# Batched x times y-transposed in groups of four heads: one 4 MB store a group in 32 KB rows, with weight tiles of 32 columns, in place of two 2 MB stores in 16 KB rows with 64 columns

## The chip, the cores and the metric

The kernel runs on one NeuronCore of a Trainium2 chip. The metric is the device time of one execution in microseconds (us), lower is better; the time before is the median of 5 runs. The profile is of one of those executions. The core has a TensorE (PE, with its weight loads as PEld), VectorE (DVE), ScalarE (ACT), GpSimd (POOL), SyncE (SP, which here only issues DMAs) and 16 DMA engines that move data between the device memory (HBM) and the on-chip memory (SBUF). PE writes to PSUM, from where DVE or ACT copy to SBUF.

## The reference

```python
batch, n_heads, seq_t, seq_s, channels = 8, 12, 512, 512, 64
x: (8, 12, 512, 64) float32      # b h t c
y: (8, 12, 512, 64) float32      # b h s c

def reference(x, y):
    return np.einsum('bhtc,bhsc->bhts', x, y).astype(np.float32)
```

For each of the 96 heads it is a 512 x 64 matrix times a 64 x 512 matrix. The inputs are 25.2 MB together, the output 100.7 MB.

## The kernel before

The 96 heads are taken in 24 groups (NG) of four heads (G = 4). In memory a group of x, y or of the output is one contiguous block. It is cut over the 128 partitions so that partition p holds rows 16p to 16p + 15 (R = 16) of the group's 4 x 512 rows: 32 partitions (Q = 32) for each head, 16 rows in each. For x and y that is 4 KB a partition (xv, yv).

Loads: `load(g)` (L51 to L56) issues two DMAs of 512 KB on SP, y first. The first six groups are loaded at the start (L58), the load of group g + 6 is issued when `prepare(g)` runs (L73). The load pool has 6 buffers for each input.

`prepare(g)` (L64 to L98) is a generator that is advanced step by step between the tiles of the group before. POOL casts y to bf16 and writes every row twice, side by side (L68), and casts x to bf16 (L72). PE transposes y in 16 blocks of 128 x 128 (L81); because of the doubled rows, partitions 0 to 63 and 64 to 127 of the result hold the same channels. The two halves are copied from PSUM to yT with the order of columns changed so that the s index runs contiguously (L87 on DVE, L89 on ACT): the source is read with a stride. x is transposed in 8 blocks of two rows each (L93), so that a block k has the channels of row 2k on partitions 0 to 63 and those of row 2k + 1 on 64 to 127. The copy to xT (L94, DVE) interleaves blocks i and i + 4 as neighbouring columns, the index e, so that 64 neighbouring columns of xT are 32 partitions' rows of one head, two rows each. These are the weight tiles of the product.

The product (L106 to L130) runs for each group over two pairs of heads (hp) and in each over four steps i2. In a step four matmuls fill one PSUM tile pm of 128 x 1,024 f32: for both heads of the pair (h2) and both row parities (par), a matmul of 64 channels x 64 weight columns x 512 moving columns. `par` selects partitions 0 to 63 or 64 to 127 of xT and yT as input, and the half of pm's columns; h2 selects 64 of pm's partitions. Each of the four is thus in another quarter of the PE array. pm is then copied to the output tile ot, by ACT for even i2 (L123) and DVE for odd (L125). There are 3 buffers for pm.

ot has 8 rows (I) x 512 f32, 16 KB, a partition: a pair of heads fills all 128 partitions. The pool has 8 buffers. A filled ot is stored by one DMA of 2 MB on SP in rows of 16 KB (L130); the first ot of the kernel and the last one (`edge`) are stored in two DMAs of 1 MB, in runs of 8 KB, as soon as each half is filled (L128).

The tile framework sets the semaphores. All DMAs go through SP's queue in the order of the program: for each group two loads, then its stores. Eight semaphores take turns for the DMAs, so that a DMA is issued only when the eighth before it has landed.

Of the kernel before, what the change touches and what calls it, by code (L numbers as in the profile page):

```python
# [1 line left out]

# [5 lines left out]


@with_exitstack  # L10
def kernel(
    ctx: ExitStack,
    tc: tile.TileContext,
    x: bass.AP,
    y: bass.AP,
    out: bass.AP,
):

    nc = tc.nc
    B, H, T, C = x.shape
    _, _, S, _ = y.shape
    P = 128
    G = 4
    Q = P // G
    R = T // Q
    NG = B * H // G
    K = R // 2  # L30
    HP = 2
    I = R // 2
    fp32 = mybir.dt.float32
    bf16 = mybir.dt.bfloat16
    assert C * 2 == P and S == T and R == 16

    xv = x.rearrange("b h t c -> (b h t c)").rearrange("(g p n) -> g p n", p=P, n=R * C)
    yv = y.rearrange("b h t c -> (b h t c)").rearrange("(g p n) -> g p n", p=P, n=R * C)
    ov = out.rearrange("b h t s -> (b h t s)").rearrange("(g a p n) -> g a p n", a=G // HP, p=P, n=I * S)

    const = ctx.enter_context(tc.tile_pool(name="const", bufs=1))
    lpool = ctx.enter_context(tc.tile_pool(name="lpool", bufs=6))
    bpool = ctx.enter_context(tc.tile_pool(name="bpool", bufs=2))
    tpool = ctx.enter_context(tc.tile_pool(name="tpool", bufs=2))
    opool = ctx.enter_context(tc.tile_pool(name="opool", bufs=8))
    ptpool = ctx.enter_context(tc.tile_pool(name="ptpsum", bufs=2, space=bass.MemoryType.PSUM))
    pmpool = ctx.enter_context(tc.tile_pool(name="pmpsum", bufs=3, space=bass.MemoryType.PSUM))

    loaded = {}

    def load(g):  # L51
        xs = lpool.tile([P, R * C], fp32)
        ys = lpool.tile([P, R * C], fp32)
        nc.sync.dma_start(ys, yv[g])
        nc.sync.dma_start(xs, xv[g])
        loaded[g] = (xs, ys)  # L56

    for g in range(6):  # L58
        load(g)

    ident = const.tile([P, P], bf16)
    make_identity(nc, ident)

    def prepare(g, made):  # L64

        xs, ys = loaded.pop(g)
        yb = bpool.tile([P, R, 2, C], bf16)
        nc.gpsimd.tensor_copy(  # L68
            yb, ys.rearrange("p (r c) -> p r c", c=C).unsqueeze(2).to_broadcast([P, R, 2, C])
        )  # L70
        xb = bpool.tile([P, R * C], bf16)
        nc.gpsimd.tensor_copy(xb, xs)  # L72
        if g + 6 < NG:  # L73
            load(g + 6)
        yield
        yT = tpool.tile([P, G * Q, R], bf16)
        xT = tpool.tile([P, K // 2, P, 2], bf16)
        for half in range(2):
            pt = ptpool.tile([P, K, P], bf16)
            for k in range(K):  # L80
                nc.tensor.transpose(  # L81
                    pt[:, k, :], yb[:, half * K + k].rearrange("p a c -> p (a c)"), ident
                )
            dst = yT[:, :, half * K:(half + 1) * K]
            src = pt.rearrange("p k n -> p n k")
            if half == 0:
                nc.vector.tensor_copy(dst, src)  # L87
            else:
                nc.scalar.activation(dst, src, mybir.ActivationFunctionType.Copy)  # L89
            yield  # L90
        pt = ptpool.tile([P, K, P], bf16)
        for k in range(K):
            nc.tensor.transpose(pt[:, k, :], xb[:, k * P:(k + 1) * P], ident)  # L93
        nc.vector.tensor_copy(  # L94
            xT.rearrange("p i n e -> p i e n"), pt.rearrange("p (e i) n -> p i e n", e=2)
        )
        made[g] = (xT, yT.rearrange("p n k -> p (n k)"))
        yield  # L98

    made = {}  # L100
    for _ in prepare(0, made):
        pass
    for g in range(NG):
        xT, yT = made.pop(g)
        steps = prepare(g + 1, made) if g + 1 < NG else iter(())
        for hp in range(G // HP):  # L106
            ot = opool.tile([P, I, S], fp32)
            edge = (g == 0 and hp == 0) or (g == NG - 1 and hp == 1)
            for i2 in range(I // 2):
                if i2 % 2 == 0:  # L110
                    next(steps, None)
                pm = pmpool.tile([P, 2, S], fp32)
                for h2 in range(HP):
                    h = hp * HP + h2
                    for par in range(2):
                        nc.tensor.matmul(  # L116
                            pm[h2 * 64:(h2 + 1) * 64, par, :],
                            xT[par * C:(par + 1) * C, i2, h * Q:(h + 1) * Q, :].rearrange("c q e -> c (q e)"),
                            yT[par * C:(par + 1) * C, h * S:(h + 1) * S],
                            start=True, stop=True,  # L120
                        )
                if i2 % 2 == 0:
                    nc.scalar.activation(ot[:, 2 * i2:2 * i2 + 2, :], pm, mybir.ActivationFunctionType.Copy)  # L123
                else:
                    nc.vector.tensor_copy(ot[:, 2 * i2:2 * i2 + 2, :], pm)  # L125
                if edge and i2 % 2 == 1:
                    a, b = (2 * i2 - 2) * S, (2 * i2 + 2) * S
                    nc.sync.dma_start(ov[g, hp][:, a:b], ot.rearrange("p r s -> p (r s)")[:, a:b])  # L128
            if not edge:
                nc.sync.dma_start(ov[g, hp], ot.rearrange("p r s -> p (r s)"))  # L130


# [1 line left out]
_INS = ['x', 'y']  # L134
_OUTS = [((8, 12, 512, 512), 'float32')]


# [23 lines left out]
```

## Time and profile before

| | us |
|---|---|
| median of 5 runs | 306.88 (306.79 to 308.15) |
| the profiled execution, its own time | 306.79 |
| its span, first to last instruction | 305.0 |
| PE busy, 1,344 matmuls and transposes | 159.8 |
| PEld busy, 1,344 weight loads | 83.8 |
| DVE busy | 172.8 |
| ACT busy | 117.3 |
| POOL busy | 70.5 |
| DMA: 126.04 MB, mean over the span | 413 GB/s |
| stores of 2 MB: 46, issue to landing | 25.0 median |
| stores of 1 MB: 4, issue to landing | 23.5 median |
| loads of 512 KB: 48, issue to landing | 24.5 median |

Busy time is the time in which an engine executed something, as a sum over the span; engines work beside each other, so the rows add up to more than the span. The page divides the span into 40 slices and gives each engine's busy share in tenths, and the same for the mean of the 16 DMA engines. "share of 16 engines" for a queue is the time that its packets took, over 16 times the span. In the groups of instructions the columns are busy time, mean time of one in ns, and the idle time just before them with what ended most of it.

### The profile page before, as it was taken

To read this page: it belongs to the slowest core of one execution; us is meant where nothing else is said; L and a number is where in the kernel's file an instruction comes from. 1 tells how busy PE (TensorE), PEld (TensorE's weight loads), DVE (VectorE), ACT (ScalarE), POOL (GpSimd) and SP (SyncE) were. 2 spreads that over 40 slices of the span, in tenths; PEclk is the share of its full clock that TensorE was granted. 3 is DMA by queue.
4 is the path that set the end of the run, shared out by engine and by line. 5 is a ranking of instruction groups with operands and counts; after the bars stand their busy time and mean duration, and the time that the engine had idled before them with its cause. 6 is when DMAs were issued, how large, how long until landed. Compare 5 with 4: busy or idle time off the path is not lost.

```text
span 305.0 us, 3408 instructions
## 1 busy us (share of the span) xinstructions
PE 159.8 (52%) x1344; PEld 83.8 (27%) x1344; DVE 172.8 (57%) x144; ACT 117.3 (38%) x121; POOL 70.5 (23%) x54
## 2 busy tenths in 40 slices
PE   1887678666554665636656466465654854300000
PEld 1453334342332323413224133242332421100000
DVE  0799999766464664646646565465564775410000
ACT  1487767434234342343323523335234453400000
POOL 4864335132130321303213213032130000000000
PEclk9966666655555555555555555555555555555555
DMA  7999999999999999999999999999999999999991
GB/s 284 416 386 440 423 420 434 414 440 410 421 434 435 417 434 415 439 414 425 435 424 427 431 423 430 430 421 439 417 438 425 431 428 432 434 425 436 423 411 68
DMA packets 14127, 126.04 MB, mean 413 GB/s; under 512 B 1568, under 2 KB 1568, under 8 KB 7712
## 3 DMA queue, kind: packets, MB, share of 16 engines
q1 hardware_dynamic: 14112, 125.84, 98.0%
q8 instruction: 10, 0.16, 0.2%
q14 instruction: 5, 0.04, 0.0%
HBM read 25.17 MB, written 100.66 MB: 413 GB/s over the span
## 4 chain that ended last, share of the span: by engine, by line
DMA 78%; DVE 6%; PE 1%; ACT 1%; POOL 1%; issue 0%; SPq 0%; ACTq 0%
DMA out_dram<-ot 77%; DVE ot L125 4%; DVE xT L94 1%; DVE yT L87 1%; DMA ys<-in_y_dram 1%; PE pm L116 1%; ACT ot L123 1%; POOL yb L68 1%; PE pt L81 0%; PE pt L93 0%; SPq L130 0%; ACTq L123 0%
## 5 line engine op out<-in xcount | busy, mean ns | idle before, releaser
L125 DVE COPY ot<-pm 128x1024 f32<-128x1024 f32 x96 | 116.3, 1220 | 78.7 <-DMA out_dram<-ot 58.8
L123 ACT ACTIVATE ot<-pm 128x1024 f32<-128x1024 f32 x96 | 94.4, 1022 | 142.0 <-DMA out_dram<-ot 129.5
L116 PE MATMUL pm<-yT,xT 64*64 64x512 bf16 x768 | 97.6, 572 | 85.2 <-ACT ot L123 69.6
L68 POOL CAST yb<-ys 128x2048 bf16<-128x2048 f32 x24 | 45.4, 1893 | 135.4 <-DMA ys<-in_y_dram 114.2
L116 PEld LDWEIGHTS <-xT 64*64 64x64 bf16 x768 | 31.0, 120 | 135.2 <-issue 119.6
L81 PE MATMUL pt<-ident,yb 128*128 128x128 bf16 x384 | 45.7, 287 | 15.7 <-DVE xT L94 9.4
L81 PEld LDWEIGHTS <-yb 128*128 128x128 bf16 x384 | 36.4, 133 | 25.2 <-issue 18.6
L94 DVE COPY xT<-pt 128x1024 bf16<-128x1024 bf16 x24 | 31.2, 1299 | 9.5 <-PE pt L93 9.5
L87 DVE COPY yT<-pt 128x1024 bf16<-128x1024 bf16 x24 | 29.1, 1213 | 7.2 <-PE pt L81 7.2
L72 POOL CAST xb<-xs 128x1024 bf16<-128x1024 f32 x24 | 25.0, 1040 | 21.9 <-PE pt L93 21.9
L93 PE MATMUL pt<-ident,xb 128*128 128x128 bf16 x192 | 25.3, 287 | 6.1 <-ACT yT L89 4.5
L89 ACT ACTIVATE yT<-pt 128x1024 bf16<-128x1024 bf16 x24 | 24.7, 1028 | 7.0 <-PE pt L81 6.3
L93 PEld LDWEIGHTS <-xb 128*128 128x128 bf16 x192 | 17.4, 123 | 22.2 <-issue 21.9
L89 ACT ACT_TABLE_LOAD x1 | 1.3, 1283 | 0.7 <-PEq L145 0.7
masks.py:199 POOL TENSOR_SCALAR_AFFINE_SELECT ident<-ident 128x128 bf16<-128x128 bf16 x1 | 0.3, 292 | 0.1
masks.py:197 POOL MEMSET ident<- 128x128 bf16 x1 | 0.2, 204 | 0.3 <-POOLq L145 0.3
L145 POOL MEMSET const-float32-0.0<- 128x1 f32 x1 | 0.1, 98 | 0.2 <-issue 0.2
L145 POOL MEMSET const-bfloat16-1.0<- 128x1 bf16 x1 | 0.1, 101 | 0.0
L145 POOL MEMSET const-uint8-127<- 128x1 uint8 x1 | 0.1, 101 | 0.0
L145 POOL MEMSET const-float32-1.0<- 128x1 f32 x1 | 0.1, 98 | 0.0
## 6 DMA issues: line engine op xcount, KB each, us to landing
out_dram<-ot SPq DMA_DIRECT2D x46, 2048.0 KB, 25.0
ys<-in_y_dram SPq DMA_DIRECT2D x24, 512.0 KB, 24.6
xs<-in_x_dram SPq DMA_DIRECT2D x24, 512.0 KB, 24.4
out_dram<-ot SPq DMA_DIRECT2D x4, 1024.0 KB, 23.5
```

The lines of the kernel that those rows point to most:

```text
L68: nc.gpsimd.tensor_copy(yb, ys.rearrange("p (r c) -> p r c", c=C).unsqueeze(2).to_broadcast([P, R, 2, C]))
L72: nc.gpsimd.tensor_copy(xb, xs)
L81: nc.tensor.transpose(pt[:, k, :], yb[:, half * K + k].rearrange("p a c -> p (a c)"), ident)
L87: nc.vector.tensor_copy(dst, src)
L89: nc.scalar.activation(dst, src, mybir.ActivationFunctionType.Copy)
L93: nc.tensor.transpose(pt[:, k, :], xb[:, k * P:(k + 1) * P], ident)
L94: nc.vector.tensor_copy(xT.rearrange("p i n e -> p i e n"), pt.rearrange("p (e i) n -> p i e n", e=2))
L116: nc.tensor.matmul(pm[h2 * 64:(h2 + 1) * 64, par, :], xT[par * C:(par + 1) * C, i2, h * Q:(h + 1) * Q, :].rearrange("c q e -> c (q e)"), y ...
L123: nc.scalar.activation(ot[:, 2 * i2:2 * i2 + 2, :], pm, mybir.ActivationFunctionType.Copy)
L125: nc.vector.tensor_copy(ot[:, 2 * i2:2 * i2 + 2, :], pm)
L145: nc = _bacc.Bacc("TRN2", target_bir_lowering=False, num_devices=1)
```

## The change

The output of a group is handled as one tile instead of two. ot is now 16 rows x 512 f32, 32 KB, a partition, for all four heads; its pool has 4 buffers in place of 8, the same bytes. A group's 4 MB are stored by one DMA in rows of 32 KB; in the first group and in the last one four DMAs of 1 MB in runs of 8 KB store a quarter each as soon as it is filled.

To fill such a tile, a step k makes two rows of every partition: pm's partitions 32h to 32h + 31 hold head h. So eight matmuls fill one pm, four heads times two parities, each with 64 channels x 32 weight columns x 512 moving columns. There are 8 steps a group as before, with the same number of copies on ACT and DVE, and the same places for the steps of `prepare`. The interleaving of xT falls away: xT is a plain copy of the transposed blocks. The copies of the transposed y, which read PSUM with a stride and write contiguous rows, are the same lines in both kernels.

```diff
-    HP = 2
-    I = R // 2
...
-    ov = out.rearrange("b h t s -> (b h t s)").rearrange("(g a p n) -> g a p n", a=G // HP, p=P, n=I * S)
+    ov = out.rearrange("b h t s -> (b h t s)").rearrange("(g p n) -> g p n", p=P, n=R * S)
...
-    opool = ctx.enter_context(tc.tile_pool(name="opool", bufs=8))
+    opool = ctx.enter_context(tc.tile_pool(name="opool", bufs=4))
...
-        xT = tpool.tile([P, K // 2, P, 2], bf16)
+        xT = tpool.tile([P, K, P], bf16)
...
-        nc.vector.tensor_copy(
-            xT.rearrange("p i n e -> p i e n"), pt.rearrange("p (e i) n -> p i e n", e=2)
-        )
+        nc.vector.tensor_copy(xT, pt)
...
-        for hp in range(G // HP):
-            ot = opool.tile([P, I, S], fp32)
-            edge = (g == 0 and hp == 0) or (g == NG - 1 and hp == 1)
-            for i2 in range(I // 2):
-                if i2 % 2 == 0:
-                    next(steps, None)
-                pm = pmpool.tile([P, 2, S], fp32)
-                for h2 in range(HP):
-                    h = hp * HP + h2
-                    for par in range(2):
-                        nc.tensor.matmul(
-                            pm[h2 * 64:(h2 + 1) * 64, par, :],
-                            xT[par * C:(par + 1) * C, i2, h * Q:(h + 1) * Q, :].rearrange("c q e -> c (q e)"),
-                            yT[par * C:(par + 1) * C, h * S:(h + 1) * S],
-                            start=True, stop=True,
-                        )
...
-                if edge and i2 % 2 == 1:
-                    a, b = (2 * i2 - 2) * S, (2 * i2 + 2) * S
-                    nc.sync.dma_start(ov[g, hp][:, a:b], ot.rearrange("p r s -> p (r s)")[:, a:b])
-            if not edge:
-                nc.sync.dma_start(ov[g, hp], ot.rearrange("p r s -> p (r s)"))
+        ot = opool.tile([P, R, S], fp32)
+        edge = g == 0 or g == NG - 1
+        for k in range(K):
+            if k % 2 == 0:
+                next(steps, None)
+            pm = pmpool.tile([P, 2, S], fp32)
+            for h in range(G):
+                for par in range(2):
+                    nc.tensor.matmul(
+                        pm[h * Q:(h + 1) * Q, par, :],
+                        xT[par * C:(par + 1) * C, k, h * Q:(h + 1) * Q],
+                        yT[par * C:(par + 1) * C, h * S:(h + 1) * S],
+                        start=True, stop=True,
+                    )
+            if k % 2 == 0:
+                nc.scalar.activation(ot[:, 2 * k:2 * k + 2, :], pm, mybir.ActivationFunctionType.Copy)
+            else:
+                nc.vector.tensor_copy(ot[:, 2 * k:2 * k + 2, :], pm)
+            if edge and k % 2 == 1:
+                a, b = (2 * k - 2) * S, (2 * k + 2) * S
+                nc.sync.dma_start(ov[g][:, a:b], ot.rearrange("p r s -> p (r s)")[:, a:b])
+        if not edge:
+            nc.sync.dma_start(ov[g], ot.rearrange("p r s -> p (r s)"))
```

More of the change, by code (lines that the diff above doesn't have):

```diff
@@ L105 @@
         steps = prepare(g + 1, made) if g + 1 < NG else iter(())
-        for hp in range(G // HP):
-            ot = opool.tile([P, I, S], fp32)
-            edge = (g == 0 and hp == 0) or (g == NG - 1 and hp == 1)
-            for i2 in range(I // 2):
-                if i2 % 2 == 0:
-                    next(steps, None)
-                pm = pmpool.tile([P, 2, S], fp32)
-                for h2 in range(HP):
-                    h = hp * HP + h2
-                    for par in range(2):
-                        nc.tensor.matmul(
-                            pm[h2 * 64:(h2 + 1) * 64, par, :],
-                            xT[par * C:(par + 1) * C, i2, h * Q:(h + 1) * Q, :].rearrange("c q e -> c (q e)"),
-                            yT[par * C:(par + 1) * C, h * S:(h + 1) * S],
-                            start=True, stop=True,
-                        )
[L122 to L125, printed above, removed]
-                if edge and i2 % 2 == 1:
-                    a, b = (2 * i2 - 2) * S, (2 * i2 + 2) * S
-                    nc.sync.dma_start(ov[g, hp][:, a:b], ot.rearrange("p r s -> p (r s)")[:, a:b])
-            if not edge:
-                nc.sync.dma_start(ov[g, hp], ot.rearrange("p r s -> p (r s)"))
```

## The prediction

> **What bounds the kernel now.** I read the page first: the time slices, the queues and the chain that ended last.
>
> ```profile
> span 305.0 us, 3408 instructions
> ...
> DMA  7999999999999999999999999999999999999991
> ...
> q1 hardware_dynamic: 14112, 125.84, 98.0%
> q8 instruction: 10, 0.16, 0.2%
> ...
> DMA 78%; DVE 6%; PE 1%; ACT 1%; POOL 1%; issue 0%; SPq 0%; ACTq 0%
> ...
> L125 DVE COPY ot<-pm 128x1024 f32<-128x1024 f32 x96 | 116.3, 1220 | 78.7 <-DMA out_dram<-ot 58.8
> L123 ACT ACTIVATE ot<-pm 128x1024 f32<-128x1024 f32 x96 | 94.4, 1022 | 142.0 <-DMA out_dram<-ot 129.5
> ```
>
> The 16 DMA engines (one ring each) are full in every slice but the first and the last, and DVE and ACT wait for stores. So the end is set by what each ring must carry, not by an engine. Then the stretches after the last computation (columns: PE, PEld, DVE, ACT, POOL busy, clock, DMA share, GB/s):
>
> ```profile
> 274.00:280.00 6.00, 0.00 (x0) 0.00 (x0) 0.00 (x0) 0.00 (x0) 0.00 (x0) 0.50 1.01 434
> 292.00:298.00 6.00, 0.00 (x0) 0.00 (x0) 0.00 (x0) 0.00 (x0) 0.00 (x0) 0.50 0.90 380
> 298.00:301.00 3.00, 0.00 (x0) 0.00 (x0) 0.00 (x0) 0.00 (x0) 0.00 (x0) 0.50 0.24 101
> 301.00:305.00 4.00, 0.00 (x0) 0.00 (x0) 0.00 (x0) 0.00 (x0) 0.00 (x0) 0.50 0.04 16
> ```
>
> All rings run at 434 GB/s, then drop out one by one; after 301 us about one is left (0.04 of 16). The rings do not end together, and the last one sets the time. The landings of the last store say the same: first ring 296.9 us, median 298.3, last 304.0. Over the stores before, the distance from first to last ring grows: 1.8 us at 48, 3.5 at 97, 4.5 at 150, 5.4 at 200, 7.1 at 265, and then stays at 7.1.
>
> Why does one ring lag? The trace records each DMA packet with size, start and duration. A 4 KB packet takes 159 ns (5,451 of 6,144 exactly), 8 KB 309 (505 of 512), 16 KB 611 (5,560 of 5,888); the next one on the ring starts 155.3, 305.5 and 607.2 ns after its predecessor. A DMA ends in a 9 ns semaphore packet, about 5 ns of ring time. The other 16 KB packets are nearly all 614 to 676 ns long and follow each other at 0.63 us: at any time one ring carries them. Their lengthening (4 KB ones included, the few above 90 ns left out) against the instructions that began in the same time:
> 30 to 50 us: 772 ns, 402 instructions (1.92 ns each); 100 to 200: 2,812 ns, 1,107 (2.54); 250 to 270: 375 ns, 138 (2.72); 270 to 300: 3 ns, 3. From 30 to 290 us it is 7.0 us, which is the lag of the last ring. So one ring gives up about 2 ns per instruction that the core executes, and nothing once the core stands still though stores go on.
>
> **The change, part by part.**
>
> *Stores.* Before, a ring carries 48 loads x 8 packets x 0.1553 = 59.6 us, 46 stores x 8 x 0.6072 = 223.5, 4 edge stores x 8 x 0.3055 = 9.8, and 98 semaphore packets, 0.5: 293.4 us. With its start at 1.8 to 2.1 us and the slow first packets that fits the first rings' end of 296.5. After: 22 stores of 4 MB, 8 packets of 32 KB each, and 8 edge stores of 1 MB with 8 KB runs. No row shows a 32 KB packet. From 4 to 8 KB two halves cost 5.1 ns more than one whole, from 8 to 16 KB 3.8 ns; 32 KB then starts its successor after 2 x 607.2 - 3.9 = 1,210.5 ns. Bounds: 1,206.7 (bytes alone, at the 8-to-16 KB slope) and 1,214.4 (two packets). So 22 x 8 x 1.2105 = 213.05, 64 x 0.3055 = 19.55, 78 semaphores 0.4: with the loads 292.6 us, a gain of **0.7 us** (0.0 to 1.4).
>
> The Trainium skill, "DMA: Bandwidth & Descriptors", section "Anatomy of one DMA", gives each DMA (there one issued from GpSimd; here SP issues them) a fixed cost of about 2 us; 20 DMAs fewer would then bring an estimated 40 us. The rows speak against it here: with DMAs queued behind each other the ring pays some 5 ns between two, not microseconds.
>
> *Matmuls.* 768 matmuls of 64 columns become 1,536 of 32, each with its weight load, so +768 and +768 instructions; -20 DMA issues: +1,516. First their time on PE, which is not on the path:
>
> ```profile
> 143.95 1.56 PE L116 MATMUL pm<-yT,xT 64*64 64x512 bf16 x12 [1.70 <-ACT ot L123]
> 145.89 0.64 PE L116 MATMUL pm<-yT,xT 64*64 64x512 bf16 x4 [0.39 <-DVE ot L125]
> ```
>
> Four matmuls in four corners of the array run together (0.64 us against some 0.57 for one), and three such sets take 1.56, so a set adds 0.52 at most. Eight together would be about 0.75 us a pm tile; run four at a time, 1.04. A group has 8 pm tiles and 24 transposes (3 x 8, 1.05 us each at most: 3.2 us), so 9.2 to 11.5 us. A group's bytes, 5.24 MB at 427 GB/s (the middle stretches), take 12.3 us. Hidden either way; it decides only from (12.3 - 3.2) / 8 = 1.14 us a tile.
>
> Then their count, which is on the path, since the last ring pays for it. Price per instruction: the nearest row by density is 30 to 50 us, 20 a us (the changed middle will have some 193 in 12.3 us, 16 a us; now it is 11): 1.92 ns. Ends: 1.16, the slope of a line with a constant term through the two rows 30-50 and 100-200, and 2.72. I take 1.92: 1,516 x 1.92 = **+2.9 us** (1.8 to 4.1; 0 if the loss follows not instructions but, say, evacuated tiles, see below). A gain is excluded, as nothing else falls in number.
>
> The Trainium skill, "SBUF — State Buffer" section "SBUF: two separate sides", says that a DMA cannot be slowed by a compute instruction, the ports being disjoint. By it this term would be nothing and the sum 306.4. The rows disagree: 2,812 ns lost from 100 to 200 us, 3 ns from 270 to 300 us.
>
> *Instruction fetch.* The q8 row: 10 packets of 16 KB (0.94 us each by the records) for 2,688 PE instructions. 1,536 more make 5.7 packets, 5.4 us over 16 rings: **+0.3 us** on the last ring on average, 0 to 0.94 if it catches none or one.
>
> *xT copy.* L94 writes every second element now, 1,299 ns; after, contiguous on both sides. Bounds: the f32 copy of equal count, 1,220 ns, and half of it. At most 24 x 0.69 = 17 us off DVE, which idles 132 us of 305 behind stores: nothing on the path. If DVE were the bound it would be worth all of that. The strided y copies (L87, L89) are not touched.
>
> *Order and buffers.* Nothing is moved past a queue; SP issues two loads, then one store instead of two. Eight DMA semaphores are in use, so a DMA is issued when the eighth before it has landed: now 4 stores and 4 loads in flight (10.5 MB, the 25 us to landing), after at least 2 stores and 4 loads (10.5 MB). A new buffer is needed every 12.3 us, when the last ring has landed the store four groups back; queued behind that are some 11 MB, 27 us for the last ring and 27 less its lag of 10, 17 us, for the first. Filling takes some 8 us (ACT and DVE in turn; with PE at its dearest 11.5). The rings stay full: nothing. Start: the first 16 loads fill the rings to about 22 us; the first store is ready at 13.2 us (DVE's first copy ends 13.2), and 4 matmuls more per tile delay it by under 1 us: nothing. The end: the last DMA is a 1 MB edge store in both.
>
> *Sum.* The profiled run took 306.79 us (span 305.0, 1.8 around it); the median of five is 306.88, the same. 306.79 - 0.7 + 2.9 + 0.3 = **309.3 us**, 0.8% slower.
>
> **Rivals.**
>
> *Not slower: the lost time does not follow PE instructions* (306.79 - 0.7 + 0.3 = 306.4). For it: before, every evacuation goes with four matmuls, so counts of evacuations, busy time and instructions rise and fall together and the rows cannot part them. Against: with 79% of all instructions on PE, 2 ns each needs no further cause. It decides from a price below (0.9 + 0.4) / 1,516 = 0.9 ns. Chance 0.22.
>
> *PE becomes the bound.* If 32-column tiles ran two at a time, a pm tile takes 2.08 us and a group 16.6 + 3.2 = 19.8: 24 x 19.8 = 475 us. Against: four corners run together in the rows. With it I count rings running dry by coarse buffers: 2 us for each of 22 groups would be 350 us; it begins only when filling takes over 17 us. Together 0.05.
>
> *32 KB runs do much better:* the memory side gains from long runs, a 32 KB packet at 1,190 ns: 176 x 0.0205 = 3.6 us more, 305.7. Against: from 8 to 16 KB the price per byte hardly moved. Chance 0.07. *The change doesn't do it:* 32 KB runs cut into two packets give 309.9, within the forecast.
>
> **How the numbers follow.** Forecast 0.66, own range 307.8 to 311.0 (price 1.16 to 2.72, fetch 0 to 0.94). Rivals 0.22, 0.05, 0.07. Range 306.2 to 311.0: it takes in the rival at 306.4. 0.3% (0.92 us) is about what a measurement of this kernel can tell from no change. Slower: 0.66 + 0.05 and a little of the 0.22, 0.72; same 0.19; faster 0.09.
>
> **What would show it.** Queue rows: 1,248 semaphore packets instead of 1,568, q8 with 15 or 16 packets. 32 KB packets of about 1,214 ns. PE matmul groups of eight within 0.6 to 1.1 us, PE still idle behind stores. The distance between first and last landing at the end near 10 us instead of 7.1, and the first rings done near 296. If that distance stays at 7, the price per instruction was wrong; if the DMA share dips in the middle, the rings ran dry.

## The result and the profile after

The changed kernel takes 309.14 us (median of 43 runs, 308.90 to 310.67), the kernel before 307.22 us beside it (80 runs, 306.68 to 311.04). The ratio is 1.0045, 95% interval 1.0032 to 1.0058: slower by 0.45%, or 1.4 us. The lowest times differ by 2.2 us. Medians and ranges in this document are of all runs, while the ratios leave out runs more than 1.5% above the fastest of their kernel, so a median and a ratio can move by different amounts.

From the page of the changed kernel: span and slices, queues, the chain that ended last, and three groups.

```profile
span 307.3 us, 4865 instructions
...
DMA  7999999999999999999999999999999999999970
...
q1 hardware_dynamic: 11232, 125.83, 96.8%
q8 instruction: 16, 0.26, 0.3%
...
DMA 72%; DVE 11%; PE 2%; issue 1%; ACT 1%; POOL 1%; SPq 0%; DVEq 0%; ACTq 0%
...
L118 DVE COPY ot<-pm 128x1024 f32<-128x1024 f32 x96 | 114.8, 1220 | 91.3 <-DMA out_dram<-ot 77.2
L116 ACT ACTIVATE ot<-pm 128x1024 f32<-128x1024 f32 x96 | 96.0, 1022 | 143.4 <-DMA out_dram<-ot 120.6
...
L91 DVE COPY xT<-pt 128x1024 bf16<-128x1024 bf16 x24 | 16.5, 688 | 17.0 <-PE pt L90 17.0
```

The rings are full from the second slice on as before, DVE and ACT still wait for stores, and the instruction queue fetched 16 blocks instead of 10. The xT copy fell from 1,299 to 688 ns and brought nothing. The stretches after the computation, with the columns as before (busy time of the five engines, clock, DMA share, GB/s):

```profile
274.00:280.00 6.00, 0.00 (x0) 0.00 (x0) 0.00 (x0) 0.00 (x0) 0.00 (x0) 0.50 0.99 426
292.00:298.00 6.00, 0.00 (x0) 0.00 (x0) 0.00 (x0) 0.00 (x0) 0.00 (x0) 0.50 0.85 359
298.00:301.00 3.00, 0.00 (x0) 0.00 (x0) 0.00 (x0) 0.00 (x0) 0.00 (x0) 0.50 0.23 96
301.00:304.00 3.00, 0.00 (x0) 0.00 (x0) 0.00 (x0) 0.00 (x0) 0.00 (x0) 0.50 0.06 27
304.00:307.30 3.30, 0.00 (x0) 0.00 (x0) 0.00 (x0) 0.00 (x0) 0.00 (x0) 0.50 0.04 15
```

From 301 us on one ring works alone (a sixteenth is 0.06), and now until 306. The landings of the last store: first ring 295.8, median 298.7, last but one 300.9, last 306.3; before 296.9, 298.3, 301.5 and 304.0. So the first ring is done 1.1 us earlier and the last one 2.3 us later; the distance went from 7.1 to 10.6 us. The records give 1,213 ns for a 32 KB packet (2,643 of 2,816). The small lengthenings after 30 us (those of the prediction, up to 90 ns for a packet of 4 to 16 KB and up to 180 ns for one of 32 KB) add up to 10.2 us against 7.0.

PE in the middle of the changed kernel:

```profile
162.37 1.54 PE L109 MATMUL pm<-yT,xT 64*32 64x512 bf16 x24 [4.53 <-ACT ot L116]
164.34 2.40 PE L109 MATMUL pm<-yT,xT 64*32 64x512 bf16 x32 [0.43 <-DVE ot L118]
167.22 0.63 PE L109 MATMUL pm<-yT,xT 64*32 64x512 bf16 x8
```

Eight matmuls take what four took (0.63 us; 24 in 1.54 where 12 took 1.56). Before each such stretch PE stands idle for some 4.5 us behind ACT, which waits for a store.

### The profile page after: what moved, and what is told of

Same layout as the page of the kernel before. It is cut to its first block, busy times and chain, and to the rows that moved or that the text cites. A ratio compares the mean times of both kernels' runs of the same rounds, so it can differ in the third digit from the quotient of the medians.

```text
span 307.3 us, 4865 instructions
## 1 busy us (share of the span) xinstructions
PE 158.7 (52%) x2112; PEld 80.8 (26%) x2112; DVE 157.4 (51%) x144; ACT 119.2 (39%) x121; POOL 70.5 (23%) x54
## 4 chain that ended last, share of the span: by engine, by line
DMA 72%; DVE 11%; PE 2%; issue 1%; ACT 1%; POOL 1%; SPq 0%; DVEq 0%; ACTq 0%
DMA out_dram<-ot 71%; DVE ot L118 8%; DVE yT L84 2%; PE pm L109 1%; DMA ys<-in_y_dram 1%; DVE xT L91 1%; ACT ot L116 1%; PE pt L78 1%; POOL yb L65 1%; PE pt L90 0%; ACT yT L86 0%; SPq L123 0%; DVEq L118 0%; ACTq L116 0%
## 5 line engine op out<-in xcount | busy, mean ns | idle before, releaser
L118 DVE COPY ot<-pm 128x1024 f32<-128x1024 f32 x96 | 114.8, 1220 | 91.3 <-DMA out_dram<-ot 77.2
L116 ACT ACTIVATE ot<-pm 128x1024 f32<-128x1024 f32 x96 | 96.0, 1022 | 143.4 <-DMA out_dram<-ot 120.6
L109 PE MATMUL pm<-yT,xT 64*32 64x512 bf16 x1536 | 99.1, 560 | 99.2 <-ACT ot L116 83.4
L109 PEld LDWEIGHTS <-xT 64*32 64x32 bf16 x1536 | 30.1, 97 | 156.2 <-issue 143.2
L78 PE MATMUL pt<-ident,yb 128*128 128x128 bf16 x384 | 42.8, 277 | 7.7 <-POOL yb L65 6.1
L78 PEld LDWEIGHTS <-yb 128*128 128x128 bf16 x384 | 35.2, 130 | 15.8 <-issue 7.8
L84 DVE COPY yT<-pt 128x1024 bf16<-128x1024 bf16 x24 | 29.1, 1214 | 7.1 <-PE pt L78 7.1
L90 PE MATMUL pt<-ident,xb 128*128 128x128 bf16 x192 | 26.0, 280 | 5.8 <-ACT yT L86 5.1
L91 DVE COPY xT<-pt 128x1024 bf16<-128x1024 bf16 x24 | 16.5, 688 | 17.0 <-PE pt L90 17.0
L90 PEld LDWEIGHTS <-xb 128*128 128x128 bf16 x192 | 16.7, 125 | 17.9 <-issue 17.9
```

The costliest lines, as they stand in the source:

```text
L78: nc.tensor.transpose(pt[:, k, :], yb[:, half * K + k].rearrange("p a c -> p (a c)"), ident)
L91: nc.vector.tensor_copy(xT, pt)
L109: nc.tensor.matmul(pm[h * Q:(h + 1) * Q, par, :], xT[par * C:(par + 1) * C, k, h * Q:(h + 1) * Q], yT[par * C:(par + 1) * C, h * S:(h + 1) ...
L116: nc.scalar.activation(ot[:, 2 * k:2 * k + 2, :], pm, mybir.ActivationFunctionType.Copy)
L118: nc.vector.tensor_copy(ot[:, 2 * k:2 * k + 2, :], pm)
```

## The experiments

Each was run beside the kernel before on the same chip: e1 to e4 (its median 307.06 us), e5 to e8 (307.65) and e9 to e12 (307.69). Theory "count": one ring loses some 2 ns for each instruction, and the end is that ring's. Rival "size": the coarser stores or buffers cost. "Distance" is that between the first and the last ring's landing of the last store. It and all counts of packets are from one profiled run of each kernel.

**Narrow weight tiles alone** (e1_cols32).

```diff
-                    for par in range(2):
-                        nc.tensor.matmul(
-                            pm[h2 * 64:(h2 + 1) * 64, par, :],
-                            xT[par * C:(par + 1) * C, i2, h * Q:(h + 1) * Q, :].rearrange("c q e -> c (q e)"),
+                    for j in range(2):
+                        for par in range(2):
+                            nc.tensor.matmul(
+                                pm[h2 * 64 + 32 * j:h2 * 64 + 32 * j + 32, par, :],
+                                xT[par * C:(par + 1) * C, i2, h * Q + 16 * j:h * Q + 16 * j + 16, :].rearrange("c q e -> c (q e)"),
```

> The kernel before with nothing changed but the matmuls: each of 64 weight columns is cut into two of 32, so 768 matmuls and 768 weight loads more, same stores, same buffers, same bytes. Theory 'count' (the last ring pays about 2 ns for each instruction): +2.9 us over before (1.8 to 4.1), the distance between the first and the last ring's landing of the last store 10 us instead of 7.1, the first ring done near 297 as before. Rival 'size' (the changed kernel's loss comes from its 4 MB stores, 32 KB runs or 4 buffers): no change, distance 7.1.

Measured: 309.83 us (309.63 to 310.15) against 307.06; ratio 1.0068 (1.0044 to 1.0093); lowest against lowest +2.9. Distance 10.2; first ring 296.7, as before (296.9); small lengthenings 9.7 us. Its stretches at the end:

```profile
301.00:304.00 3.00, 0.00 (x0) 0.00 (x0) 0.00 (x0) 0.00 (x0) 0.00 (x0) 0.50 0.06 25
304.00:307.90 3.90, 0.00 (x0) 0.00 (x0) 0.00 (x0) 0.00 (x0) 0.00 (x0) 0.50 0.04 17
```

Same bytes, same packets, same buffers, and one ring works on alone as in the changed kernel. By the lowest times the whole loss, and more, comes from the cut of the matmuls: 2.9 us for 1,536 instructions, 1.9 ns each, instruction fetch included.

**Coarse stores and buffers alone** (e2_4mb_16k).

```diff
-    opool = ctx.enter_context(tc.tile_pool(name="opool", bufs=8))
+    opool = ctx.enter_context(tc.tile_pool(name="opool", bufs=4))
...
+        ot2 = opool.tile([P, G // HP, I, S], fp32)
...
-            ot = opool.tile([P, I, S], fp32)
+            ot = ot2[:, hp]
...
+            elif hp == 1:
+                nc.sync.dma_start(
+                    ov[g].rearrange("a p n -> p a n"), ot2.rearrange("p a r s -> p a (r s)")
+                )
```

> The kernel before with the two output tiles of a group in one buffer (4 buffers of 32 KB in place of 8 of 16 KB) and, in the 22 middle groups, one DMA of 4 MB with two runs of 16 KB in each partition; matmuls, weight tiles and edge stores of 1 and 2 MB as before. Theory 'count': no change (-0.1 us, 22 DMAs fewer), distance 7.1. Rival 'size', where the coarser stores and buffers cost: +1 to +2 us.

Measured: lowest 306.75, the same as before (306.74), but the runs spread to 311.89, median 310.15; ratio 1.0046 (1.0010 to 1.0082). The profiled run (309.42) ends otherwise than e1:

```profile
298.00:301.00 3.00, 0.00 (x0) 0.00 (x0) 0.00 (x0) 0.00 (x0) 0.00 (x0) 0.50 0.42 180
301.00:304.00 3.00, 0.00 (x0) 0.00 (x0) 0.00 (x0) 0.00 (x0) 0.00 (x0) 0.50 0.23 98
304.00:307.60 3.60, 0.00 (x0) 0.00 (x0) 0.00 (x0) 0.00 (x0) 0.00 (x0) 0.50 0.06 27
```

Several rings are late (0.23 of 16 is nearly four), the last two at 306.0 and 306.5. After 30 us the records show 82 load packets lengthened by over 90 ns, 33 in the profiled run of the kernel before, which was one of its fastest. So neither theory was whole: the floor (the lowest time) does not move, as "count" has it, but the ratio is clear of no change and rings also fall behind by something else; the times say that it comes more often here.

**Long runs undone** (e5_after_16k): the changed kernel with two DMAs in place of each 4 MB store.

```diff
-            nc.sync.dma_start(ov[g], ot.rearrange("p r s -> p (r s)"))
+            for a in (0, R * S // 2):
+                b = a + R * S // 2
+                nc.sync.dma_start(ov[g][:, a:b], ot.rearrange("p r s -> p (r s)")[:, a:b])
```

> The changed kernel with each 4 MB store of the middle groups issued as two DMAs of 2 MB, each with runs of 16 KB: 32-column tiles, 4 buffers and instruction count stay. It undoes the 32 KB runs alone. Theory 'count': over the changed kernel +0.7 us (0.0 to 1.0), all of it on every ring, so 309.7 against before 306.9; first ring's last landing 296.7 instead of 295.8, distance as in the changed kernel (10.6). Rival 'size' (the long runs or big stores are what costs): it falls back by 1 us or more.

Measured: 310.34 us (310.14 to 310.56), lowest against the changed kernel's lowest +1.2; first ring 296.6 instead of 295.8, distance 11.1. The first ring moved by 0.8 us as the sum had it, the last one by 1.3, and the lowest time by more than the 0.0 to 1.0 us expected. The long packets are a gain, and a little more than their own time on the last ring; why more is not shown.

**More instructions on POOL** (e3_pool_extra, then e6_pool_extra32 with half as many). 64 memsets of one column in each group, 8 behind every copy; then 32 behind the casts:

```diff
+        for _ in range(32):
+            nc.gpsimd.memset(scratch, 0.0)
```

> The kernel before with 64 memsets of one column (128x1 f32, about 0.1 us each) added on POOL in each group, 1,536 in all; POOL is idle three quarters of the time, nothing waits for them but the casts behind them, at most 0.8 us. Theory 'count' in its wide form (any instruction costs, whatever its engine): +2.9 us (1.8 to 4.1) and a distance of about 10 us. Narrow form (only matmuls and weight loads cost, by what they read): no change, distance 7.1.

> The kernel before with 32 memsets of one column on POOL behind the two casts of each group, 768 in all (0.155 us each in the run with 64, so 5 us a group beside 2.9 us of casts, in a period of 12.3: POOL is not the bound). Wide form (every instruction costs the last ring about 2.2 ns): +1.7 us, distance 8.8. Narrow form (only matmuls and weight loads): 0, distance 7.1.

Measured: 375.1 us (ratio 1.2185, 1.2145 to 1.2224) and 312.4 us (1.0158, 1.0104 to 1.0212). Both miss their question. The program put the memsets before casts that were needed, POOL became the bound and the rings ran dry; a late ring then catches up (distance 1.7 and 2.9 us). The longest waits of the second:

```profile
ACT ot L126 <- PE pm L119: 118.6, 37, 18.2
DVE ot L128 <- PE pm L119: 75.7, 20, 16.0
PEld L119 <- issue: 69.5, 124, 2.9
PEld L84 <- POOL scratch L75: 62.6, 8, 16.1
```

The transposes wait for POOL's memsets, and the copies for PE, no more for stores. Only its start can be used: from 30 to 130 us, with full rings, the lengthenings were 4.4 us for some 1,580 instructions, 2.8 ns each, with half of the added ones on POOL. That speaks for any instruction, but it does not settle it.

**One ring left out at the end** (e4_tail120).

```diff
+                    parts = [(0, P)] if g == 0 else [(0, 120), (120, P)]
+                    for p0, p1 in parts:
+                        nc.sync.dma_start(ov[g, hp][p0:p1, a:b], ot.rearrange("p r s -> p (r s)")[p0:p1, a:b])
```

> The kernel before with the two 1 MB edge stores of the last tile each cut in two: partitions 0 to 119, then 120 to 127. The sizes 120 and 8 go over fewer rings than 16 if the number of rings is the largest divisor up to 16 (15 and 8), which leaves one ring out of the last 2 MB. If the end is set by one lagging ring and that ring is the one left out: it gives up 16 packets of 8 KB, 4.9 us, the next rings (2.5 us ahead of it) take over, and the time falls by 1.9 us (1.5 to 2.5). If another ring lags: +0.6 us at most, since the second DMA adds two 8 KB packets to eight rings. If the rings are even and the lag is no cause: no change or a little slower.

Measured: 311.87 us (308.48 to 314.30), ratio 1.0106 (1.0072 to 1.0139). The split did go over 15 and 8 rings (46 semaphore packets instead of 32), but its 8 KB packets took up to 1,234 ns instead of 309. It came out slower than any of the three cases expected. The price of such a split hides the answer; which ring is the late one stays open.

**The DMAs alone** (e7_dma_only, e8_dma_only_32k): no instruction between the DMAs, 2 MB and 4 MB stores.

> All the DMAs of the kernel before in the same order and sizes, with the computation left out: the loads are never read and the stores send tiles that were set to zero once. It shows the rings with the core standing still. Theory 'count': the lag is gone, distance under 2 us, the first ring near 296.5 as before, last near 298, so 300 us (299 to 301.5). Rival 'ring' (one ring is slower by itself, from the memory's side): distance about 7, 306 us.

> The same with the DMAs of the changed kernel (22 stores of 4 MB in 32 KB runs, 8 of 1 MB). Theory 'count' with the gain of the long packets by themselves: 0.7 to 1.0 us under the run with 2 MB stores, about 299.2 us; distance under 2 us. Rival 'size': not faster than it.

Measured: 309.92 us (306.66 to 310.82) and 307.84 us (301.74 to 309.08). The first is where theory "count" fell as the only cause. Half of it held: 5,870 of 5,888 packets of 16 KB took 611 ns (before 5,560), the small lengthenings were 1.0 us instead of 7.0. Yet one ring was 11.5 us late (columns here: DVE, POOL, clock, DMA share, GB/s):

```profile
292.00:298.00 6.00, 0.00 (x0) 0.00 (x0) 1.00 0.76 322
298.00:301.00 3.00, 0.00 (x0) 0.00 (x0) 1.00 0.13 55
301.00:304.00 3.00, 0.00 (x0) 0.00 (x0) 1.00 0.09 38
304.00:309.00 5.00, 0.00 (x0) 0.00 (x0) 1.00 0.05 20
```

Fourteen rings were done by 297.2 us, one at 302.9, the last one at 308.2. Its distance grew from 2.9 us at 55 to 11.5 at 199, while loads ran, then stood. Chained by start and end, the records put some 9 us of lengthened packets on that ring, mostly loads of 4 KB. In the second run the first ring ended at 295.7 instead of 296.7, again the gain of the long packets, but the run was expected at 299.2 us and its times lie too far apart for a verdict.

**Without the later loads** (e9_dma_six_loads: DMAs alone; e10_six_loads: with the computation).

```diff
-        xs, ys = loaded.pop(g)
+        xs, ys = loaded[g % 6]
...
-        if g + 6 < NG:
-            load(g + 6)
```

> The run with the DMAs of the kernel before alone (computation left out), and with the loads of groups 6 to 23 left out as well. That run kept a lag of 11.5 us on one ring although its 16 KB packets were all 611 ns; its lag grew only between 55 and 200 us, in which loads ran among the stores, and single 4 KB packets took 400 to 1,100 ns. New theory 'slow loads' (a second cause: a late ring's load packets are slow now and then): 36 loads x 8 x 0.1553 = 44.7 us less on every ring, no growth of the lag after the loads, distance under 2.5 us, so 253 to 255 us with runs within 1 us of each other. Rival (a ring falls behind by its stores or their issue): distance 6 us or more, 259 us and up, runs spread as widely as with loads (306.7 to 310.8).

> The kernel before with all its computation, but the loads of groups 6 to 23 left out: those groups compute on the first six groups' data. Instructions on PE, DVE, ACT and POOL stay the same. Theory 'count' plus 'slow loads': bytes 44.7 us less, the instruction lag stays: distance 7 to 8 us, time 261 to 263 us, and the spread of the runs, 4 us for the kernel before, shrinks to under 1 us. If the instructions cost nothing on a ring: distance under 2.5 us, 255 us. If the spread is not from the loads: it stays at 3 to 4 us.

Measured: 256.67 us (255.99 to 257.37) and 263.05 us (262.89 to 263.12). The ends, first of the DMAs alone, then with the computation:

```profile
250.00:252.00 2.00, 0.00 (x0) 0.00 (x0) 1.00 1.01 422
252.00:254.50 2.50, 0.00 (x0) 0.00 (x0) 1.00 0.17 69
```

```profile
255.00:258.00 3.00, 0.00 (x0) 0.00 (x0) 0.00 (x0) 0.00 (x0) 0.00 (x0) 0.50 0.06 25
258.00:261.30 3.30, 0.00 (x0) 0.00 (x0) 0.00 (x0) 0.00 (x0) 0.00 (x0) 0.50 0.04 15
```

Without loads and without instructions all rings end within 0.9 us, and no load packet after 30 us is slow because there is none. With the instructions back, one ring is 7.7 us late, and the six runs lie within 0.23 us, where those of the kernel before beside them spread over 3.9 us even without its longest one (306.70 to 310.58). The two are 6.4 us apart. With e7 and the kernel before there are four cases: loads and computation (distance 7.1), loads alone (11.5), computation alone (7.7), neither (0.9). They separate the causes: the computation makes a lag of one ring that hardly varies from run to run, the loads make one that does, and the spread. That it is the number of instructions in the computation that counts is e1's part. The first run took 2 us more than expected; 788 of its 5,888 store packets of 16 KB were lengthened by up to 25 ns each (4.7 us in all), with hardly an instruction in the program. Since all its rings still ended together, these did not gather on one ring. So small lengthenings are not a mark of instructions by themselves; a lag of one ring that grows with them is.

**Loads on another queue** (e11_loads_act): `nc.scalar.dma_start` in place of `nc.sync.dma_start` in `load`.

> The kernel before with its loads issued on ACT's DMA queue instead of SP's, so that load packets go between store packets rather than in blocks of 16 behind them. Theory 'slow loads' with a late ring alone in a block of loads: the spread of the runs shrinks and the median comes near the lowest, 306.8; the lowest does not move, since instructions set it. Rival: reads among writes are slow whenever they come, so each load packet costs more: +1 us or more. The issues take some 0.35 us x 48 on ACT, which idles 142 us.

Measured: 307.24 us (307.04 to 307.87) against 307.69 (306.70 to 312.17) beside it; ratio 0.9975 (0.9950 to 1.0001). The spread shrank to 0.8 us, with 8 slow load packets instead of 33, as expected. The lowest, which should have stood, rose by 0.3, and the ratio is not clear of no change.

**Fewer PE instructions, same result** (e12_half_transposes).

```diff
+        for k in range(K):
+            nc.tensor.transpose(pt[:, k, :], yb[:, k * P:(k + 1) * P], ident)
+        yT4 = yT.rearrange("p n (k e) -> p n k e", e=2)
+        for e in range(2):
+            src = pt[e * C:(e + 1) * C].rearrange("p k n -> p n k")
+            nc.vector.tensor_copy(yT4[0:C, :, :, e], src)
+            nc.scalar.activation(yT4[C:P, :, :, e], src, mybir.ActivationFunctionType.Copy)
```

> The kernel before with fewer PE instructions and the same result: y is transposed once, in 8 blocks instead of 16 doubled ones, and four copies of 64 partitions (two DVE, two ACT) put each block on both halves of the partitions. 384 PE instructions fewer, 48 copies more: -336. Theory 'count': the lowest times fall by 0.7 us to 306.0, distance 6.4 in a run without slow loads on the last ring; the spread upward stays, so the median falls less. Rival (the copies' extra 1.2 us a group on DVE and ACT counts): +0.3 us or more, from the start, where DVE is busy all the time.

Measured: lowest 305.99 us against 306.70 beside it, as expected; distance 6.6 in the profiled run. Its runs reach 311.97, median 308.57, ratio 1.0005 (0.9964 to 1.0045), where a small fall was expected. DVE's busy time rose from 173 to 204 us without cost to the lowest time. By the lowest times the instruction term goes down as it goes up, 2.1 ns each, with 9 blocks of instructions fetched instead of 10; the small lengthenings fell by 0.2 us only (7.0 to 6.8), so the records support that figure weakly. What lies above it is taken to be the other lag.

## Why the prediction was right, step by step

*The bound.* Full rings, the last one sets the end: as predicted, also in the changed kernel. One reading was too neat: the 7.0 us of lengthenings from 30 to 290 us were taken for the whole lag of 7.1, of which 1.8 us stood already at 48 us by the prediction's own row. The lag grew by 5.3 us in that time, so not all lengthenings became lag.

*Stores, -0.7 us.* The 32 KB packet took 1,213 ns where about 1,214 was expected. The first ring gained 1.1 us between the two profiles, 0.8 when e5 undid it. Right, slightly too small.

*Matmul time, hidden.* Eight tiles cost what four cost; the estimate of 0.75 us a tile was too high (0.51), and nothing depended on it. The Trainium skill, "TensorE: Matmul & The Clock Gate", section "Measured speedup vs the span model", has a set of tiles last one matmul and about 4 ns for each further tile, so an estimated 16 ns more for eight than for four. The trace agrees to some 0.03 us (0.63 us for eight, 0.64 for four).

*xT copy, nothing.* It fell to 688 ns, within the bounds of 610 to 1,220, and nothing on the path moved. Of DVE's 132 idle us only 58.8 were behind stores by the table of waits, not all of them; the conclusion does not need it.

*Matmul count, +2.9 us.* e1 measured +2.8 between medians, +2.9 between lowest times and +0.68% by the ratio, 2.1 us; e12 by its lowest time and the pair e9 and e10 found the term from the other side. This was the step that decided, and the rival "the lost time does not follow PE instructions" (306.4 us) falls with e1, where the evacuated tiles stayed the same. What carries the loss is not shown. Nor is it shown that instructions of other engines cost as much: e1 and e12 changed those of PE almost alone. And since every timed run here comes with a span and a granted clock, all were recorded; that the recording of each instruction is itself what reaches the ring is a rival that no run here excludes. The Trainium skill, "SBUF — State Buffer", section "SBUF: two separate sides", holds that a compute instruction cannot slow a DMA; the pair e9 and e10 differs by 6.4 us, so some path of the running program does reach a ring, which need not be the port that the page speaks of.

*Fetch, +0.3 us.* 16 blocks were fetched, as counted. e1's 2.9 us holds this term and the count together, where the sum had 3.2 for the two. The small lengthenings, from which the prediction took its price, rose by 2.6 us in e1 (7.0 to 9.7), so that price may have been a little too high; which ring caught the fetches is not shown.

*The other rivals.* PE did not become the bound (0.63 us for eight matmuls), 32 KB runs were not much better (1,213 ns a packet, not 1,190), and they were not cut in two (2,816 packets of 32 KB).

*The sum, 309.3 us.* The median is 309.14, and that it is so near is partly luck: the terms that the sum had too large stand where late loads lift the median above the lowest time (308.90). Against the kernel before, 2.5 us were forecast, the medians differ by 1.9, the lowest times by 2.2, and the ratio says 1.4 (1.0 to 1.8). The step that failed is the reading that "one ring gives up about 2 ns per instruction" is the lag: it is one of two. A ring that is late by slow loads ends, by the spread of the runs, at a different place in each run. In the kernel before, the instruction ring ends early enough that such a ring often comes last, and the runs reach from 306.7 to 311.0. In the changed kernel the instruction ring ends 2.2 us later and mostly comes last: three quarters of its runs lie between 308.9 and 309.3. The later ring of the two sets the time, so the mean moves by less than the floor. An estimate from the times: raise each of the 80 runs of the kernel before to at least 308.9 (the lowest of the changed kernel) or 309.1 us (about its median), and their mean rises by 1.2 or 1.4 us. e10 supports the two lags; that they make the whole difference between 2.2 and 1.4 is worked out, not shown.

*Buffers and order, nothing.* No dip of the DMA share; e2's floor did not move. That e2's runs spread upward, with 82 slow load packets in the profiled one where the changed kernel has 37 with the same buffers, is not explained.

## What to carry to other kernels

When all DMA engines are full, look at the landings of the last transfer engine by engine: the mean share hides the one that ends last, and here a term of 2 ns per instruction on it outweighed a gain of every packet. Price a cut into smaller matmuls by their number too, even where PE idles. Compare lowest times and spreads beside medians: two lags that compete for the end make a change look smaller than its own step.

## What was not expected of the hardware

The DMAs alone were no faster than the whole kernel: 306.7 to 310.8 us, with one ring 11.5 us behind its fellows by slow 4 KB load packets among stores, where without loads the rings stay within 0.9 us. Issuing the loads on a second queue took most of that spread away in the whole kernel (0.8 us instead of 3.9 or more). A kernel with both the loads on ACT's queue and half the transposes was not tried.
